# Gathers three jobs ahead with four row buffers, expert weights in natural row order, last job's row loads on Pool's queue, a warm-up for the first gather

## The chip, the cores and the metric

The kernel runs on one core of one Trainium2 chip. The metric is the time of one execution in device microseconds (us); the median of three runs of the kernel before is 736.16 us (733.53 to 736.91). PE is the tensor engine (PEld its weight loads), DVE the vector engine, ACT the scalar engine, POOL the general-purpose engine, SP the engine that only issues transfers. Each engine works off its own instructions in order.

## The reference: one diffusion layer with a mixture of experts

The layer takes 512 tokens of width 1024 and 256 context tokens. First comes a mixer (a combined input projection, a gated short convolution and a gated linear attention, an output projection, a post-norm residual). Then each token goes to two of sixteen experts. What the change touches is the second half:

```python
for e in range(N_EXPERTS):
    act = jax.nn.silu(tok @ w1[e]) * (tok @ w3[e])
    out = out + combine[:, e:e + 1] * (act @ w2[e])
...
x = post_norm_residual(x, hier_moe(modulate(x, sh2, sc2), *moe_w), g2, ln2_g[l], ln2_b[l])
```

`w1` and `w3` are 1024x512 and `w2` is 512x1024 for each expert, all in 32-bit floats; `combine` is zero but for the two experts of a token. `modulate` is x * (1 + scale) + shift, column by column.

## The kernel before, in words

**Jobs.** The kernel sorts the experts by their number of tokens and works through 16 jobs. Two first jobs take up to 96 slots of experts 0 and 1, so that work can start before the sort is known; 14 more have fixed capacities by rank (256, 192, 128 three times, 96 twice, 64 three times, 32 three times, 31), run in the order of `ORDER`, which sets big and small ones in turn: by capacity 96, 96, 31, 256, 32, 192, 64, 128, 64, 128, 64, 128, 96, 96, 32, 31. A job is split into groups of up to 128 slots and each group into blocks. A block of 128 slots (`Block`) splits its weights into a high and a low part (ACT casts `whi`, DVE subtracts `wlo`) and does three products for each; smaller ones (`SmallBlock`) multiply directly in 32 bits. Counting groups there are 18 gathers, counting blocks 21 scatters (the last job has none).

**A job's steps.** `hots` builds the 0/1 matrix of tokens and slots on DVE. `prep` makes the job and calls `slots`: four small matrix products give token numbers and weights per slot, DVE turns them into indices, and an indirect DMA on Pool's queue gathers the token rows from DRAM (`tokd`) into a row buffer `gx` (line 1227). `load` transposes the rows on PE (line 1253) and applies the modulation. `hidden` multiplies with `w1` and `w3`, `gate` does silu and the product, `outputs` multiplies with `w2`, and an indirect DMA on Pool's queue adds the rows to `yd` in DRAM (`scatter`, line 1187). Two scatters both change `yd`, so each waits until the one before has landed.

**The order.** In the loop over the jobs, job n loads the next one's rows within its last hidden step, then does `gate`, then the `prep` of job n+2, then the next job's first hidden step, then its own `outputs`. So on Pool's queue a gather stands between scatters. There are three row buffers. The Tile framework turns the written order into one queue for each engine and moves independent instructions within it.

**Weights.** Each expert comes in six pieces of 1 MB, loaded by SP into a ring of twelve tiles (line 1019), so a piece is issued when the piece of two jobs before has been used, and only in order. The pieces are read with `"o (p k) n -> p (o k) n"`: partition p gets four neighbouring rows of `w1` or two of `w2`, 8 KB in one run. The rows of one product are therefore every fourth (or second) of the matrix, and the kernel compensates: `load` transposes every fourth column of `gx`, `abx` holds the modulation in that order (made by `perm` in `ada_fin` from four extra small loads `pvec`, line 545), and `gate` writes and reads in that order.

**The last job.** `last_hot`, three jobs before the end, builds what adds the last job's rows and ALPHA * `ln1_b` on PE rather than by a scatter. SP loads `ln1_b` into `l1b`, a tile of the ring `ob` of two tiles that also holds the scatters' sources (line 1556); ACT multiplies it by ALPHA (line 1557); SP copies four pieces into `obw` (line 1561), which Pool has set to zero (line 1559). `finish` then reads `yd` back into the three row buffers and one further tile, normalizes and stores.

Of the kernel before, what the change touches and what calls it, by code (L numbers as in the profile page):

```python
# [18 lines left out]
P = 128  # L19
# [35 lines left out]
WARM0, WARM1, WARM2, WARM3 = 28, 8, 16, 16  # L55
# [7 lines left out]
def layer(ctx: ExitStack, tc: tile.TileContext, a, out, dbg=None):  # L63
# [179 lines left out]
    def ada_fin(pa, parts, bank, prio, perm=None):  # L243


        s = sb.tile([P, 512], FT, name="adas", tag="as", bufs=2)
        S.copy(s, pa)
        n = len(parts)

        def columns(src, bias):  # L250
            o = bank()[:, :8 * n].rearrange("p (k q i) -> p q k i", i=2, q=n)
            for j in range(4):
                mm(o[:, :, j, :], src(j), sel[:, 0:2 * n], prio, start=True, stop=True)
            ts_ = []
            for q, (c0, hf) in enumerate(parts):
                t = sb.tile([P, 4, 2], FT, name="adac", tag="adac", bufs=4)
                V.tensor_tensor(t, o[:, q], bias(c0, hf)[:, :, None].to_broadcast([P, 4, 2]), op=OP.add)
                ts_.append(t)
            return ts_

        ts_ = columns(lambda j: s[:, j * P:(j + 1) * P], lambda c0, hf: vc(VBA + 8 * c0, hf))
        if perm:
            return ts_, lambda: columns(lambda j: s.rearrange("r (p c) -> r c p", c=4)[:, j], perm)
        return ts_

    class Ada:
# [10 lines left out]
        def fin(self, perm=None):  # L277
            return ada_fin(self.pa, self.parts, pbg, PR_ADA, perm)
# [7 lines left out]
    def ab_half(dst, sh, sc, hf, g0, b0, col=None):  # L286

        def bc2(c0):
            return (col or vc)(c0, hf)[:, :, None].to_broadcast([P, 4, 2])
# [243 lines left out]
    pvec = sb.tile([P, 4, 2, 4], FT, name="pvec", tag="wsum")  # L533
    V.memset(g4, 0.0)
    with tc.issue_after(wk_lo.ins):
        G.dma_start(wl, dview(a["w_in"], OFF_GF, [[DPROJ, P], [P * DPROJ, KC], [1, 32]]))
        for j in range(4):
            G.dma_start(g4[32 * j:32 * j + 16, :, 0:DK], a["gate_w2_fwd"][0].rearrange("r (h d) -> r h d", h=NH))
            G.dma_start(g4[32 * j + 16:32 * j + 32, :, DK:P], a["gate_w2_bwd"][0].rearrange("r (h d) -> r h d", h=NH))
        G.dma_start(gn, dview(a["gla_norm_g"], 0, [[0, P], [1, DV]]))  # L540
        G.dma_start(wr[:, :, 0:4], a["router_group_w"][0].rearrange("(k p) g -> p k g", p=P))
        G.dma_start(wr[:, :, 4:20], a["router_expert_w"][0].rearrange("(k p) g -> p k g", p=P))

        for n_, v_ in enumerate((a["b_ada"][0, 3 * D:4 * D], a["b_ada"][0, 4 * D:5 * D], a["ln1_g"][0], a["ln1_b"][0])):
            G.dma_start(pvec[:, n_], v_.rearrange("(h p c) -> p h c", h=2, c=4))
        G.dma_start(rb[:, 0:4], dview(a["router_group_b"], 0, [[0, P], [1, 4]]))
        G.dma_start(rb[:, 4:20], dview(a["router_expert_b"], 0, [[0, P], [1, 16]]))
# [33 lines left out]
    ab2 = sb.tile([P, 2, KC, 2], FT, name="ab2", tag="lg")  # L581

    abx = const.tile([P, 2, KC, 2], FT)
# [29 lines left out]
    def px(n, hf):  # L613
        return pvec[:, n, hf]

    (sh0, sc0, sh1, sc1), perm = ada.fin(lambda c0, hf: px(c0 - 3, hf))
# [281 lines left out]
    wsum = sb.tile([P, 2, 20], FT, name="wsum", tag="wsum")  # L898
# [18 lines left out]
    lg = sb.tile([P, NT, 20], FT, name="lg", tag="lg")  # L917
# [265 lines left out]
    gxs = [mo.tile([P, D], FT, name=f"gx{n}") for n in range(3)]  # L1183
# [6 lines left out]

    def every(src, c, j):

        return src.rearrange("s (p c) -> s c p", c=c)[:, j]
# [10 lines left out]
    class Group:  # L1204
# [8 lines left out]
        def slots(self):  # L1213
# [5 lines left out]
            sa = mo.tile([P, 8], FT, name="sa", tag="sa", bufs=8)[:n]  # L1219
            V.tensor_copy(sa[:, :NA], pa[:n, :NA])  # L1220
            V.scalar_tensor_tensor(sa[:, 0:1], sa[:, 2:3], dum[:n, 1:2], sa[:, 0:1], op0=OP.mult, op1=OP.add)
            idx = mo.tile([P, 1], I32, name="idx", tag="idx", bufs=8)[:n]
# [18 lines left out]
        def load(self):  # L1241
# [7 lines left out]
            for hf in range(2):  # L1249
                pt = pt_()  # L1250
                gh = self.g[:, hf * 512:(hf + 1) * 512]
                for c in range(4):
                    PE.transpose(pt[:, c * n:(c + 1) * n], every(gh, 4, c), ident[:n, :n])  # L1253
                v = pt[:, :4 * n].rearrange("p (c n) -> p c n", c=4)
                ks = slice(4 * hf, 4 * hf + 4)
                if big:
                    hi, lo = self.X
                    for c in range(4):
                        A, B = abx[:, 0, 4 * hf + c, 0:1], abx[:, 1, 4 * hf + c, 0:1]
# [6 lines left out]
                else:  # L1266
                    A, B = (abx[:, q, ks, 0:1].to_broadcast([P, 4, n]) for q in range(2))
# [4 lines left out]
    class Block:  # L1272
# [18 lines left out]
        def gate(self):  # L1291
            self.A = hi, lo = hl_tiles(4, "A")
            s_ = mo.tile([P, 512], FT, name="s", tag="s", bufs=3)
            for q in range(2):
                cs = slice(q * 256, (q + 1) * 256)

                h1, h3 = (h[:, cs].rearrange("s (p o) -> s o p", o=2) for h in self.H)
                sq = s_[:, cs].rearrange("s (o p) -> s o p", o=2)
                S.activation(sq, h1, AF.Silu)
                V.scalar_tensor_tensor(sq, h3, self.group.w, sq, op0=OP.mult, op1=OP.mult)  # L1300
                pt = pt_()
                for o in range(2):
                    PE.transpose(pt[:, o * P:(o + 1) * P], sq[:, o], ident)
# [19 lines left out]
    class SmallBlock:  # L1323
# [30 lines left out]
        def gate(self):  # L1354
# [4 lines left out]
            hs = mo.tile([P, 512], FT, name="hs", tag="s", bufs=3)  # L1359
# [109 lines left out]
    for j in seq[:NS]:  # L1469
        ohs[j] = hots(j)  # L1470
        warm(WARM2, pt_)
        prep(j)
    jobs[seq[0]].load()
    with tc.issue_after(jobs[seq[NS - 1]].last.ins):
        for g, n in zip(gxs, [FIRST] * NS + [0]):
            G.memset(g[n:], 0.0)
# [65 lines left out]
    def last_hot():  # L1542
# [7 lines left out]
        V.memset(ohl[:, :, n - 1::n], 1.0)  # L1550
# [15 lines left out]
    for n_, j in enumerate(seq):  # L1566
# [45 lines left out]
    def finish():  # L1612

        ys = gxs + [mo.tile([P, D], FT, name="yf", tag="Xl", bufs=2) for _ in range(1)]
# [121 lines left out]
```

## Time and profile before

| | us |
|---|---|
| median of 3 runs | 736.16 |
| the profiled execution | 739.21 |
| its span, first to last instruction | 737.4 |
| PE busy | 648.9 (88%) |
| DVE busy | 408.0 (55%) |
| ACT busy | 250.5 (34%) |
| POOL busy | 103.9 (14%) |

A busy PE is not a PE at its peak: the ends of pipelined products are modelled, and the clock that PE is granted has two levels, 1.2 and 2.4 GHz (a mean of 0.929 of the full one here). The first 265 us are the mixer, the experts' products run from about 344 to 707 us, `finish` takes the rest. In rows of the timeline the columns are start, duration, engine, line, operation, output and inputs, shape, count, and in brackets how long the engine sat idle before it and what ended that.

### The profile page before, as it was taken

How to read it: one execution, taken by the hardware profiler on the slowest of the kernel's cores; microseconds unless marked ns; L12 is line 12 of the kernel's file. 1: busy time of each engine (PE TensorE's matmuls, PEld its weight loads, DVE VectorE, ACT ScalarE, POOL GpSimd, SP SyncE). 2: the span in 40 equal slices, each digit the busy share in tenths (PEclk: the TensorE clock that was granted, in tenths of full speed). 3: DMA queues.
4: the chain of work that ended last, by engine and by line, in shares of the span. 5: the costliest groups of instructions: out<-in, count | busy, mean ns of one | idle time of the engine just before them, and what ended most of it. 6: DMA issues, size and time to landing. Idle time of an engine off the chain costs nothing.

```text
span 737.4 us, 10628 instructions
## 1 busy us (share of the span) xinstructions
PE 648.9 (88%) x3966; PEld 429.0 (58%) x3966; DVE 408.0 (55%) x1008; ACT 250.5 (34%) x417; POOL 103.9 (14%) x106
## 2 busy tenths in 40 slices
PE   5899999989999999996996898999678978999564
PEld 4465688778887787774443576554444634544321
DVE  7436741685976759558415557456346657312036
ACT  2437712458532325141023444244323453001001
POOL 2330000000000100035103202100210111103102
PEclk8799989999999999997798899899897989999788
DMA  8995955362122098353569798857995989616963
GB/s 302 382 307 179 319 194 172 115 199 88 57 84 89 14 364 335 115 170 132 203 255 405 290 366 275 252 230 244 373 403 176 395 300 335 212 61 227 398 224 116
DMA packets 52984, 172.49 MB, mean 234 GB/s; under 512 B 4477, under 2 KB 17933, under 8 KB 40642
## 3 DMA queue, kind: packets, MB, share of 16 engines
q1 hardware_dynamic: 46130, 157.31, 57.5%
q0 software_dynamic: 5440, 11.27, 7.0%
q10 hardware_dynamic: 1360, 3.21, 1.1%
q8 instruction: 32, 0.52, 0.3%
q14 instruction: 22, 0.18, 0.1%
HBM read 159.88 MB, written 13.50 MB: 235 GB/s over the span
## 4 chain that ended last, share of the span: by engine, by line
PE 57%; DMA 17%; DVE 10%; issue 8%; ACT 5%; POOL 1%; ACTq 0%; SPq 0%; DVEq 0%; POOLq 0%
PE pb L144 22%; PE mm L144 19%; DMA yd<-ob,idx 7%; DMA gx<-tokd,idx 6%; PE gl L144 3%; PE pt L1253 2%; DVE wlo L398 2%; PE bg L146 2%; PE po L144 2%; PE tp L154 1%; DMA x<-in_x_dram 1%; ACT whi L396 1%; DMA raw<-in_w_ada_dram 1%; DVE gg L640 1%; PE bg L160 1%
## 5 line engine op out<-in xcount | busy, mean ns | idle before, releaser
L398 DVE TENSOR_TENSOR wlo<-raw,whi 128x1024 fp32r<-128x1024 f32 x68 | 82.3, 1223 | 62.6 <-ACT whi L396 62.1
L396 ACT CAST whi<-raw 128x1024 fp32r<-128x1024 f32 x68 | 70.7, 1049 | 79.6 <-PE pb L144 50.1
L144 PE MATMUL pb<-ew,xt 128*32 128x256 f32 (+1 forms) x480 | 73.7, 495 | 1.4 <-DVE xt L1270 1.2
L1187 POOL DMA_INDIRECT yd<-ob,idx x21 | 33.9, 1614 | 143.7 <-DVE ob L1388 50.4
L1253 PE MATMUL pt<-ident,gx 128*128 128x128 f32 (+3 forms) x144 | 24.8, 325 | 31.7 <-DMA gx<-tokd,idx 31.7
L144 PE MATMUL pb<-ew,at 128*32 128x256 f32 (+1 forms) x384 | 51.4, 477 | 0.9 <-DVE at L1371 0.5
L144 PE MATMUL pb<-whi,Xh 128*128 128x512 f32 x96 | 42.2, 439 | 6.2 <-ACT Xh L1264 6.2
L1363 ACT COPY hs<-pb 128x256 f32<-128x256 f32 x24 | 8.3, 374 | 114.4 <-PE pb L144 114.4
L144 PE MATMUL mm<-hhi,whi 128*128 128x512 f32 x112 | 44.7, 409 | 2.5 <-ACT hhi L375 2.2
L144 PE MATMUL pb<-raw,xt 128*32 128x256 f32 (+1 forms) x288 | 38.8, 480 | 8.2 <-DMA raw<-in_expert_w_dram 8.2
L1253 PEld LDWEIGHTS pt<-ident,gx 128*128 128x128 f32 (+3 forms) x144 | 21.3, 215 | 39.0 <-issue 28.9
L144 PE MATMUL mm<-hhi,wlo 128*128 128x512 f32 x112 | 43.8, 403 | 0.1
L1227 POOL DMA_INDIRECT gx<-tokd,idx x18 | 20.1, 1114 | 164.1 <-issue 47.0
L144 PE MATMUL mm<-hlo,whi 128*128 128x512 f32 x112 | 42.5, 390 | 0.0
L144 PEld LDWEIGHTS pb<-ew,xt 128*32 128x32 f32 (+1 forms) x480 | 22.4, 127 | 33.7 <-issue 26.2
L144 PE MATMUL pb<-whi,Xl 128*128 128x512 f32 x96 | 41.1, 428 | 0.0
L144 PE MATMUL pb<-wlo,Xh 128*128 128x512 f32 x96 | 41.0, 427 | 0.0
L144 PE MATMUL mm<-wlo,hhi 128*128 128x256 f32 x128 | 37.9, 296 | 0.0
L144 PE MATMUL mm<-whi,hhi 128*128 128x256 f32 x128 | 37.9, 296 | 0.0
L144 PE MATMUL mm<-whi,hlo 128*128 128x256 f32 x128 | 37.6, 294 | 0.0
L144 PEld LDWEIGHTS pb<-ew,at 128*32 128x32 f32 (+1 forms) x384 | 18.5, 125 | 28.8 <-issue 23.6
L301 POOL TENSOR_TENSOR ss<-ss,nhalf 128x4 f32<-128x4 f32 x4 | 5.4, 1358 | 192.3 <-DVE ss L300 192.3
(431 smaller groups left out, 1374.9 us busy)
## 6 DMA issues: line engine op xcount, KB each, us to landing
ew<-in_expert_w_dram SPq DMA_DIRECT2D x64, 1024.0 KB, 7.1
raw<-in_expert_w_dram SPq DMA_DIRECT2D x32, 1024.0 KB, 10.7
raw<-in_w_ada_dram SPq DMA_DIRECT2D x22, 1024.0 KB, 10.7
raw<-in_w_in_dram SPq DMA_DIRECT2D x10, 1024.0 KB, 6.3
raw<-in_w_out_dram SPq DMA_DIRECT2D x4, 1024.0 KB, 4.9
xz<-in_x_dram SPq DMA_DIRECT2D x4, 512.0 KB
ada<-in_w_ada_dram SPq DMA_DIRECT2D x2, 1024.0 KB
x<-in_x_dram SPq DMA_DIRECT2D x4, 512.0 KB, 11.3
```

What stands on the lines that cost most here:

```text
L144: return PE.matmul(o, lhsT, rhs, **kw)
L146: return PE.matmul(o, lhsT, rhs, **kw)
L154: PE.transpose(pool_tile[:, j * P:(j + 1) * P], s, ident)
L160: PE.transpose(o[:, :P], ident, ident)
L301: pows.append(G.tensor_tensor(dst, dst, nhalf[:, :dst.shape[1]], op=OP.pow))
L396: S.copy(hi, r[:, k0:k0 + step, :])
L398: lows.append(lo_eng[k0 // step].tensor_tensor(lo, r[:, k0:k0 + step, :], hi.bitcast(FT), op=OP.subtract))
L640: V.tensor_tensor_scan(g[DK:P, ::-1], mask[DK:P, :n], m[DK:P, ::-1], 0.0, op0=OP.mult, op1=OP.add)
L1187: G.indirect_dma_start(out=yd.rearrange("t (r w) -> (t r) w", r=R), out_offset=bass.IndirectOffsetOnAxis(ap=idx[:, :1], axis=0), in_=o, in ...
L1227: self.last = G.indirect_dma_start(out=self.g, out_offset=None, in_=tokd, in_offset=bass.IndirectOffsetOnAxis(ap=idx[:, :1], axis=0), **kw)
L1253: PE.transpose(pt[:, c * n:(c + 1) * n], every(gh, 4, c), ident[:n, :n])
L1363: S.copy(hs[:, cs].rearrange("s (o p) -> s o p", o=2), self.ph[:, cs].rearrange("s (p o) -> s o p", o=2))
```

## The change

Gathers: `prep` of job n+3 (was n+2) and `hots` of job n+4 (was n+3) after the `gate` of job n, also for the first jobs; four row buffers (was three). Tile counts go down: `sa` and `idx` 8 to 6, `s` 3 to 2, `sg` 2 to 1. Weight pieces: partition p gets rows p, p+128, ..., so runs of 2 KB for `w1` and `w3` and of 4 KB for `w2`; the compensation goes (`abx`, `pvec`, `perm`, `every`, the strided views in `gate`). Last job: ALPHA goes into the 0/1 matrix, and the four row pieces come straight from `ln1_b` by DMAs on Pool's queue; `finish` uses the four row buffers. Warm-up: 34 transposes on PE between the first two gathers' issue and the first `load`.

```diff
-WARM0, WARM1, WARM2, WARM3 = 28, 8, 16, 16
+WARM0, WARM1, WARM2, WARM4 = 28, 8, 16, 34
...
-        for n_, v_ in enumerate((a["b_ada"][0, 3 * D:4 * D], a["b_ada"][0, 4 * D:5 * D], a["ln1_g"][0], a["ln1_b"][0])):
-            G.dma_start(pvec[:, n_], v_.rearrange("(h p c) -> p h c", h=2, c=4))
...
-    xp = perm()
-    ab_half(abx, xp[0], xp[1], 0, 2, 3, px)
-    ab_half(abx, xp[2], xp[3], 1, 2, 3, px)
...
-        return src.rearrange("o (p k) n -> p (o k) n", p=P)
+        return src.rearrange("o (k p) n -> p (o k) n", p=P)
...
-    gxs = [mo.tile([P, D], FT, name=f"gx{n}") for n in range(3)]
+    gxs = [mo.tile([P, D], FT, name=f"gx{n}") for n in range(4)]
...
-                    PE.transpose(pt[:, c * n:(c + 1) * n], every(gh, 4, c), ident[:n, :n])
+                    PE.transpose(pt[:, c * n:(c + 1) * n], gh[:, c * P:(c + 1) * P], ident[:n, :n])
...
-            for q in range(m // 2):
-                cs = slice(q * 256, (q + 1) * 256)
-                S.copy(hs[:, cs].rearrange("s (o p) -> s o p", o=2), self.ph[:, cs].rearrange("s (p o) -> s o p", o=2))
-            sg = mo.tile([P, 4, n], FT, name="sg", tag="sg", bufs=2)
+            S.copy(hs[:, :m * P], self.ph[:, :m * P])
+            sg = mo.tile([P, 4, n], FT, name="sg", tag="sg", bufs=1)
...
+    warm(WARM4, pt_)
     jobs[seq[0]].load()
...
-        V.memset(ohl[:, :, n - 1::n], 1.0)
+        V.memset(ohl[:, :, n - 1::n], ALPHA)
...
-        l1b = mo.tile([1, D], FT, name="l1b", tag="ob", bufs=2)
-        nc.sync.dma_start(l1b, dview(a["ln1_b"], 0, [[0, 1], [1, D]]))
-        S.activation(l1b, l1b, AF.Copy, scale=ALPHA)
...
-            nc.sync.dma_start(obw[(q + 1) * n - 1:(q + 1) * n, q * w:(q + 1) * w], l1b[:, q * w:(q + 1) * w])
+            G.dma_start(obw[(q + 1) * n - 1:(q + 1) * n, q * w:(q + 1) * w], dview(a["ln1_b"], q * w, [[0, 1], [1, w]]))
...
-        if n_ + 3 < len(seq) and n_ + 3 >= NS + 2:
-            ohs[seq[n_ + 3]] = hots(seq[n_ + 3])
-        if n_ + 2 < len(seq) and n_ + 2 > NS:
-            prep(seq[n_ + 2])
+        if n_ + 4 < len(seq):
+            ohs[seq[n_ + 4]] = hots(seq[n_ + 4])
+        if n_ + 3 < len(seq):
+            prep(seq[n_ + 3])
...
-        ys = gxs + [mo.tile([P, D], FT, name="yf", tag="Xl", bufs=2) for _ in range(1)]
+        ys = gxs
```

## Rows read from the trace of the kernel before

**Rows 1.** The page's chain that ended last: shares of the span by engine.

```profile
PE 57%; DMA 17%; DVE 10%; issue 8%; ACT 5%; POOL 1%; ACTq 0%; SPq 0%; DVEq 0%; POOLq 0%
```

**Rows 2.** Stretches: length, busy us by engine, PE's granted clock, DMA share, GB/s.

```profile
500.00:635.00 135.00, 112.68 (x495) 63.30 (x492) 78.42 (x175) 48.49 (x72) 18.42 (x14) 0.91 0.89 328
635.00:684.00 49.00, 46.76 (x379) 22.09 (x377) 12.40 (x47) 5.56 (x15) 8.17 (x6) 1.00 0.44 138
684.00:707.50 23.50, 12.15 (x136) 7.41 (x134) 3.44 (x13) 1.27 (x5) 3.10 (x2) 0.78 0.96 364
```

**Rows 3.** Waits (total us, times, longest), then PE's timeline around gathers.

```profile
PE pt L1253 <- DMA gx<-tokd,idx: 31.7, 7, 7.4
...
529.02 1.22 PE L1253 MATMUL pt<-ident,gx 64*128 64x64 f32 x8 [7.36 <-DMA gx<-tokd,idx]
...
534.54 3.65 PE L144 MATMUL pb<-ew,xt 128*64 128x512 f32 x14
...
595.42 1.95 PE L1253 MATMUL pt<-ident,gx 128*128 128x128 f32 x8 [4.52 <-DMA gx<-tokd,idx]
597.30 5.71 PE L144 MATMUL pb<-ew,xt 128*64 128x512 f32 x14
```

**Rows 4.** Timeline of POOL: a scatter and the gather behind it.

```profile
516.76 1.57 POOL L1187 DMA_INDIRECT yd<-ob,idx  x1 [12.27 <-DMA yd<-ob,idx]
518.63 1.00 POOL L1227 DMA_INDIRECT gx<-tokd,idx  x1 [0.30 <-issue]
```

**Rows 5.** SP's own waits (total us, times, longest), and its timeline.

```profile
SPq L1561 <- ACT l1b L1557: 20.6, 1, 20.6
SPq L1556 <- DMA yd<-ob,idx: 19.5, 1, 19.5
...
670.58 2.81 SPq L1019 DMA_DIRECT2D ew<-in_expert_w_dram  x5
```

**Rows 6.** PE's timeline near the end of the jobs.

```profile
691.49 0.64 PE L144 MATMUL pb<-raw,xt 128*32 128x256 f32 x2 [6.95 <-DMA raw<-in_expert_w_dram]
```

**Rows 7.** The chain in order of time (start, us, what): its last scatters.

```profile
664.20 4.92 DMA yd<-ob,idx
...
699.80 7.75 DMA yd<-ob,idx
```

**Rows 8.** Transfers: landing (us), stretches as in rows 2, a queue of the page.

```profile
raw<-in_w_out_dram SPq DMA_DIRECT2D x4, 1024.0 KB, 4.9
...
DMA to landing us min/median/max: 5.0/5.0/5.0
...
30.00:34.00 4.00, 1.84 (x13) 1.20 (x11) 2.99 (x5) 1.72 (x3) 4.00 (x4) 1.00 1.05 388
435.00:439.00 4.00, 4.00 (x19) 3.19 (x18) 1.68 (x6) 0.74 (x1) 0.00 (x0) 1.00 1.02 416
...
q0 software_dynamic: 5440, 11.27, 7.0%
```

**Rows 9.** Groups by form: busy us and mean ns; then PE's timeline.

```profile
L1253 PEld LDWEIGHTS pt<-ident,gx 128*128 128x128 f32 x48 | 8.5, 218 | 18.9 <-issue 18.4 <-DVE Xl L1196 0.4
L154 PEld LDWEIGHTS pt<-ident,hs 128*128 128x128 f32 x48 | 5.4, 143 | 5.1 <-ACT hs L1363 2.8 <-issue 1.0 <-DVE Xl L1196 0.7
L545 POOL DMA_DIRECT2D pvec<-in_b_ada_dram x2 | 1.4, 739 | 0.0
...
93.97 1.85 PE L146 MATMUL bg<-sel,adas 128*128 128x8 f32 x8
```

**Rows 10.** PE's timeline at the first two loads, from the warm-up before.

```profile
337.14 1.97 PE L160 MATMUL pt<-ident 128*128 128x128 f32 x16
...
344.07 1.53 PE L1253 MATMUL pt<-ident,gx 96*128 96x96 f32 x8 [4.83 <-DMA gx<-tokd,idx]
354.72 5.91 PE L144 MATMUL pb<-ew,xt 128*64 128x512 f32 x38
361.70 5.52 PE L144 MATMUL pb<-ew,xt 128*64 128x512 f32 x48
```

More of the change, by code (lines that the diff above doesn't have):

```diff
@@ L241, in ada_mm, with ada_fin @@
                start=q == 0 and half == 0, stop=last and half == 1)
-    def ada_fin(pa, parts, bank, prio, perm=None):
+    def ada_fin(pa, parts, bank, prio):
         s = sb.tile([P, 512], FT, name="adas", tag="as", bufs=2)
@@ L248, in ada_fin @@
         n = len(parts)
[L250 to L263, printed above, removed]
+        o = bank()[:, :8 * n].rearrange("p (k q i) -> p q k i", i=2, q=n)
+        for j in range(4):
+            mm(o[:, :, j, :], s[:, j * P:(j + 1) * P], sel[:, 0:2 * n], prio, start=True, stop=True)
+        ts_ = []
+        for q, (c0, hf) in enumerate(parts):
+            t = sb.tile([P, 4, 2], FT, name="adac", tag="adac", bufs=4)
+            V.tensor_tensor(t, o[:, q], vc(VBA + 8 * c0, hf)[:, :, None].to_broadcast([P, 4, 2]), op=OP.add)
+            ts_.append(t)
         return ts_
@@ L275, in add, with fin @@
                 ada_mm(self.pa, r, half, PR_ADA, len(self.parts) - 1, len(self.parts) == self.n)
-        def fin(self, perm=None):
-            return ada_fin(self.pa, self.parts, pbg, PR_ADA, perm)
+        def fin(self):
+            return ada_fin(self.pa, self.parts, pbg, PR_ADA)
     ab = sb.tile([P, 2, KC, 2], FT, name="ab")
@@ L532, in layer @@
     rb = sb.tile([P, 20], FT, name="rb")
-    pvec = sb.tile([P, 4, 2, 4], FT, name="pvec", tag="wsum")
     V.memset(g4, 0.0)
@@ L577, in layer @@
     lowC = gate_low(zcT, CT)
-    ab2 = sb.tile([P, 2, KC, 2], FT, name="ab2", tag="lg")
-    abx = const.tile([P, 2, KC, 2], FT)
+    ab2 = const.tile([P, 2, KC, 2], FT)
     gT = const.tile([P, 2, KC], FT)
@@ L897, in layer @@
     V.memset(onesf, 1.0)
-    wsum = sb.tile([P, 2, 20], FT, name="wsum", tag="wsum")
+    wsum = sb.tile([P, 2, 20], FT, name="wsum")
     for q, w_ in enumerate((wa, wr)):
@@ L916, in layer @@
         S.dma_start(yd[T:T + P, h * 512:(h + 1) * 512], zero)
-    lg = sb.tile([P, NT, 20], FT, name="lg", tag="lg")
+    lg = sb.tile([P, NT, 20], FT, name="lg")
     st1 = sb.tile([P, NT, 3, 6], FT, name="st1")
@@ L1218, in slots @@
                 mm(pa[:n, :NA], self.oh[:, i, :n], self.auxj(i), start=i == 0, stop=i == NT - 1)
-            sa = mo.tile([P, 8], FT, name="sa", tag="sa", bufs=8)[:n]
+            sa = mo.tile([P, 8], FT, name="sa", tag="sa", bufs=6)[:n]
             V.tensor_copy(sa[:, :NA], pa[:n, :NA])
             V.scalar_tensor_tensor(sa[:, 0:1], sa[:, 2:3], dum[:n, 1:2], sa[:, 0:1], op0=OP.mult, op1=OP.add)
-            idx = mo.tile([P, 1], I32, name="idx", tag="idx", bufs=8)[:n]
+            idx = mo.tile([P, 1], I32, name="idx", tag="idx", bufs=6)[:n]
             V.tensor_scalar(idx, sa[:, 0:1], sa[:, 1:2], dum[:n, 0:1], op0=OP.add, op1=OP.add)
@@ L1266, in load @@
                 else:
-                    A, B = (abx[:, q, ks, 0:1].to_broadcast([P, 4, n]) for q in range(2))
+                    A, B = (ab2[:, q, ks, 0:1].to_broadcast([P, 4, n]) for q in range(2))
                     x = self.xt[:, ks, :n]
@@ L1292, in gate @@
             self.A = hi, lo = hl_tiles(4, "A")
-            s_ = mo.tile([P, 512], FT, name="s", tag="s", bufs=3)
+            s_ = mo.tile([P, 512], FT, name="s", tag="s", bufs=2)
             for q in range(2):
                 cs = slice(q * 256, (q + 1) * 256)
[L1297 to L1300, printed above, removed]
+                S.activation(s_[:, cs], self.H[0][:, cs], AF.Silu)
+                V.scalar_tensor_tensor(s_[:, cs], self.H[1][:, cs], self.group.w, s_[:, cs], op0=OP.mult, op1=OP.mult)
                 pt = pt_()
-                for o in range(2):
-                    PE.transpose(pt[:, o * P:(o + 1) * P], sq[:, o], ident)
+                transpose4(pt, [s_[:, q * 256 + o * P:q * 256 + (o + 1) * P] for o in range(2)])
                 v = pt[:, :2 * P].rearrange("p (k t) -> p k t", k=2)
@@ L1472, in layer @@
         prep(j)
+    warm(WARM4, pt_)
     jobs[seq[0]].load()
     with tc.issue_after(jobs[seq[NS - 1]].last.ins):
-        for g, n in zip(gxs, [FIRST] * NS + [0]):
+        for g, n in zip(gxs, [FIRST] * NS + [0, 0]):
             G.memset(g[n:], 0.0)
```

14 lines of the change are left out of this document (5 added, 9 removed).

## The prediction, made before the changed kernel was run

> **What bounds the kernel now.** I began with the page's chain that ended last. PE holds 57% of it, but DMA holds 17% [rows 1], and that share is the one this change can reach: the chain written out in order of time shows DMA almost only as gathers between 339 and 630 us and as five scatters in a row at the end. So two places are in question.
>
> The first is PE's wait for gathered rows. In the list of waits, PE's transposes stood idle for gathers 31.7 us in seven waits; the timeline shows them at big and small jobs alike [rows 3]. Why the rows are late stands on Pool's queue: a scatter waited 12.27 us until the scatter before it had landed, and the gather written behind it left at 518.63 [rows 4]; PE could use its rows at 529.02 [rows 3], 10.4 us later. The gather itself asks for nothing that a job earlier wasn't known.
>
> The second is the end. SP's own waits name two of about 20 us, one for a scatter to land (line 1556 needs a tile of the ring that holds the scatters' sources) and one for ACT (line 1557, queued behind work of ACT's own), and only at 670.58 does SP go on with weights [rows 5]. These 40 us fall into the stretch 635 to 684, where PE is full at full clock and the transfers are busy 0.44 of the time; in the next stretch it is the reverse, 0.96 for the transfers and 12.15 us of PE in 23.5 [rows 2]. PE pays at 691.49: 6.95 us for weights [rows 6]. And the five scatters that close the jobs, 664.20 to 707.55, take 4.92 us at first and 8.71, 9.69, 8.82 and 7.75 us once the late weights run beside them [rows 7].
>
> **The change, part by part.** Durations are those of the profiled execution, 739.2 us (span 737.4 and 1.8 around it), which lies 3.0 us above the median of 736.16.
>
> *Gathers a job earlier.* The first wait (4.83 us, [rows 10]) stays; the others are 31.7 - 4.83 = 26.9 us. A job in this phase is some 22 us (the 135 us of the first stretch hold about six, [rows 2]). The longest remaining wait is 7.36 us, so a gather that leaves one job earlier is in time with over 10 us to spare, even behind the same scatter. I take -26.9 (between -20 and -26.9). The new wait is the one for a row buffer: with two groups in the biggest jobs, three jobs ahead hold at most three groups at once plus the one being transposed, and the buffer that is taken was transposed in the hidden step just before, so I cost it at nothing; without that cover a gather would wait for a transpose, and behind it on Pool's queue the scatter of the job in hand. The moved DVE work (one-hot matrices, indices) is the same in number. The smaller counts of `sa`, `idx`, `s` and `sg` cost at most some tenths of a microsecond in the jobs with two small blocks; I take 0.
>
> *The clock after the waits.* After the gather of 595.42 the run of 14 small products took 5.71 us against 3.65 at full clock [rows 3]: 2.1 us lost, for the eight transposes perhaps 0.8 more. Four waits are of 4.5 us or more, so about 2.5 x 4 = 10 us. Some of it will come back, since after the transposes of a big job ACT and DVE need time for the modulation and the split before PE can use them: -8 (0 to -11).
>
> *Weights in natural order.* Runs of 2 KB (64 pieces, 67.1 MB) and 4 KB (32 pieces, 33.6 MB) for runs of 8 KB. The trace has loads with 2 KB runs, of `w_out` and `w_ada`. Alone, the 1 MB of `w_out` lands in 4.9 us, and the expert load that was timed between 436 and 480 us, with 8 KB runs, in 5.0: no price. In a full stream they differ: 388 GB/s at a share of 1.05 against 416 at 1.02 [rows 8], so 370 and 408 GB/s for a full share. That makes 67.1 x (1/0.370 - 1/0.408) = 16.9 us of transfer time, and 4.2 for `w2` at half the difference: 0 to 21 us over 16 jobs. What of it lies on the path depends on the stretch: 500 to 635 us has a share of 0.89, so 120 us of transfers, plus up to 8 for its six jobs; PE without its four waits there (two of them stand in rows 3, together they are 19.4 us) and the slow clock (three of them, 7.5) would be done in 108. Transfers and PE then come out nearly equal. The ring's lead (up to two jobs) gives the transfers some slack, and in the stretch behind it they are half idle. I take +8, between 0 and +20.
>
> The Trainium skill, page "DMA: Bandwidth & Descriptors", section "Why small descriptors are slow (HBM only)", speaks against this part: each packet costs about 3 fixed cycles beside its 32-byte beats. By it 2 KB runs need 67/64 and 8 KB runs 259/256, 3.5% more time per byte; an estimate from that page is 6 us for `w1` and `w3`, less than the row's 16.9. With it the sum would be some 4 us better.
>
> *The compensation goes.* Weight loads from every fourth column take 218 ns, from neighbouring ones 143 [rows 9]: 75 ns x 144 = 10.8 us of PEld, nearly all beside PE. Eight transposes at full clock differ by some 0.1 us, 18 times: -2 (0 to -5). The second set of column products in `ada_fin` is a PE item of 1.85 us in a full stretch [rows 9]: -1.7. Four `pvec` loads of 0.74 us leave Pool, where nobody waits: 0.
>
> *The first gather.* The warm-up of 34 transposes, at the 16 in 1.97 us of the warm-up before it, takes 4.2 us and fits into the 4.83 us of idling. What it can save is the half clock after: from 345.6 to 360.6 us PE needed 15 us for 48 products that take 5.52 the second time [rows 10]; I put 2 to 3 of it down to table products and a wait for DVE between them. So 0 to -7; DVE is slow there too, so I take -4. Were the clock to fall anyway the warm-up would last twice as long: +3.
>
> *The last job's rows.* SP's 40 us of standing go, the four DMAs go to Pool's queue at 0.74 us each as `pvec` did [rows 9], at a time when Pool is idle. Weights of the last two jobs come while PE is full. PE saves 6.95 [rows 6] and, as after a gather, some 2.5 at half clock. The scatters go back to about 4.9 us plus 0.7 between them: the last three, from 677.3, when their products are ready, end at 677.3 + 3 x 5.6 = 694, or 696 by PE, against 707.55 [rows 7]. I take -12; if scatters stay at 9 us it is -3, and -14 is the most.
>
> The same page's section "Issuing engines are not separate DMA queues" says that moving a DMA to another issuing engine saves only the time to issue it. By that rule this part would be worth 2.5 us or less on SP and the sum 12 us worse. Rows 5 show what the rule leaves out: the issuing engine was held by waits of its own.
>
> **The sum.** -26.9 - 8 + 8 - 2 - 1.7 - 4 - 12 = -46.6. 739.2 - 46.6 = 692.6, and with the 3.0 us between this execution and the median 689.6: **690 us**. With every bound at its best it is about 671, at its worst (waits -20, clock 0, transfers +20, strides 0, warm-up +3, tail -3) about 734; either end needs all of them together.
>
> **The rivals.** *Transfers become the bound* (0.20). The waits go, and PE then waits for weights: +20 in place of +8, and nothing from the first gather. 690 + 12 + 4 = 706. For it: the share of 0.89 [rows 2]. Against it: PE's one long wait for weights is that of rows 6, after SP's standing.
>
> *The tail stays* (0.14). The scatters must still follow one another, and the weights still run beside them: 690 + 9 = 699.
>
> *The gathers don't come earlier* (0.05). Pool's order puts them behind scatters that wait [rows 4], or the row buffer is late. Then only the tail, the warm-up and the compensation count: 736 - 12 - 4 - 4 + 2 = 718. Against it: the gather goes with its job's place in the loop.
>
> *Slower: packets, not bytes, set the pace* (0.06). The software queue moved 5440 packets, 11.27 MB, in 7.0% of 16 engines' span [rows 8]: 826 us of engine time, 152 ns for 2.07 KB, which is 218 GB/s. If 2 KB runs went at that pace, `w1` and `w3` of the 14 later jobs (58.7 MB) would take 269 us, `w2` (29.4 MB, halfway between the rates) 94, the software queue its 52: 415 us in the 363 from the first load of rows (344.07, [rows 10]) to 707.55. That ends 52 us late: 736 + 52 = 788. It decides from a rate below about 260 GB/s on; against it stand 388 GB/s for such runs [rows 8].
>
> **How the numbers follow.** The forecast's case has 0.52; 0.03 is left for no change at all. The forecast, full transfers, the staying tail and the late gathers are all faster, 0.91. About 0.5% (3.7 us) is what a measurement here can tell from no change: within it 0.03, slower 0.06. The range runs from 675, near the best bounds, to 716, which takes in the cases of 699 and 706 with 10 us to spare and leaves out the late gathers, no change and the slow packets: 0.14, and some 0.05 below.
>
> **What would show it.** Right: PE's waits for gathers shrink to the first one, of about 0.5 to 1 us beside the warm-up; gathers stand on Pool's queue a job earlier; SP has no wait at `last_hot`, and the share in the stretch with the two jobs of 96 rises over 0.44; scatters at the end take 5 to 6 us; PEld at line 1253 about 143 ns. Wrong: waits of PE or ACT for expert weights by tens of microseconds, or a DMA share at 1.0 all through with fewer GB/s than 370 (transfers); a last chain of scatters at 9 us each (tail); gathers that still end waits (order); a clock of 0.5 after the first load in spite of the warm-up.

## The result, and the profile after

The changed kernel took **685.31 us** (median of 4 runs, 680.76 to 688.91) and the kernel before, beside it, 736.53 us (733.53 to 738.34): ratio 0.9305, interval 0.9241 to 0.9369. In a second set it was 684.72 against 734.09 us, ratio 0.9345 (0.9292 to 0.9397). The forecast was 690, with a range of 675 to 716. The sum was nearly met, but two of its terms were far off, in opposite directions, and a third has no trace behind it; the experiments below show which.

The profiled execution of the changed kernel took 688.91 us (span 687.1), and the mean granted clock rose from 0.929 to 0.955. In the page's chain by engine, DMA has half of its share of before and PE more [rows 1]:

```profile
PE 67%; DVE 13%; DMA 9%; ACT 6%; issue 2%; POOL 1%; ACTq 0%; SPq 0%; DVEq 0%
```

The gathers are gone from the list of PE's waits; it was led by 31.7 us for them [rows 3]. What leads it now (total us, times, longest):

```profile
PE pb L144 <- ACT Xh L1241: 10.3, 3, 4.6
PE py L144 <- DMA gx<-yd: 8.9, 1, 8.9
PE bg L160 <- DVE dum L1036: 4.1, 1, 4.1
```

Stretches of the changed kernel (columns as in rows 2: length, busy us of PE, PEld, DVE, ACT, POOL, PE's clock, DMA share, GB/s). The jobs end some 50 us sooner, so 600 to 640 is where 635 to 684 stood before:

```profile
380.00:500.00 120.00, 114.33 (x681) 69.90 (x682) 75.03 (x166) 49.71 (x79) 19.19 (x15) 0.93 0.91 308
500.00:600.00 100.00, 93.70 (x446) 56.37 (x444) 68.37 (x152) 41.52 (x58) 19.14 (x17) 0.97 1.05 371
600.00:640.00 40.00, 39.99 (x348) 16.39 (x344) 10.10 (x39) 4.17 (x11) 7.20 (x5) 1.00 1.04 368
640.00:660.00 20.00, 9.63 (x144) 5.21 (x136) 3.69 (x13) 1.64 (x6) 3.10 (x2) 0.90 0.73 243
```

The hole in the transfers (0.44 in 635:684, [rows 2]) is filled: share 1.04 while PE is full at full clock. For 140 us the transfers have a share of 1.04 to 1.05, the highest that these rows and rows 8 show, and PE is still busy for 0.94 and 1.00 of the two stretches. SP's timeline and Pool's show what filled it (start, duration, what, count):

```profile
600.05 21.97 SPq L1000 DMA_DIRECT2D ew<-in_expert_w_dram  x5
622.22 8.30 SPq L1000 DMA_DIRECT2D raw<-in_expert_w_dram  x4
637.04 1.24 SPq L1000 DMA_DIRECT2D ew<-in_expert_w_dram  x2
```

```profile
557.57 1.02 POOL L1204 DMA_INDIRECT gx<-tokd,idx  x1 [14.06 <-DVE cmp L1637]
562.45 1.56 POOL L1168 DMA_INDIRECT yd<-ob,idx  x1 [3.86 <-DVE ob L1293]
565.27 2.09 POOL L1529 DMA_DIRECT2D obw<-in_ln_b_dram  x4 [0.30 <-POOL obw L1527]
```

The last weights leave at 637.04; before, SP still had five loads and more to send at 670.58 [rows 5]; the four row loads cost Pool 2.09 us at a place where it is idle. PE's timeline answers to rows 3 and 10:

```profile
336.88 0.85 PE L1230 MATMUL pt<-ident,gx 96*128 96x96 f32 x8 [1.06 <-DVE oh L1160]
522.09 3.65 PE L144 MATMUL pb<-ew,xt 128*64 128x512 f32 x14
530.34 0.79 PE L144 MATMUL pb<-whi,Xh 128*128 128x512 f32 x1 [4.60 <-ACT Xh L1241]
```

Ahead of the first load PE stands for 1.06 us, put down to DVE (4.83 us before, put down to the gather). The 14 small products behind a gather take 3.65 us, the time at full clock. But at 530.34 PE waits 4.60 us for ACT's split of the rows: part of the gathers' wait has moved one step on in the big jobs (10.3 us in all, 6.2 before).

The whole stretch of the experts, from the first load of rows to the landing of the last scatter (columns as in rows 2), in the kernel before, in the changed kernel, and in a second profile of the changed kernel (r1_after):

```profile
344.07:707.55 363.48, 315.29 (x1916) 175.78 (x1916) 176.79 (x440) 105.26 (x178) 60.54 (x48) 0.91 0.77 280
336.88:656.23 319.35, 299.25 (x1916) 166.16 (x1916) 174.60 (x435) 103.60 (x169) 62.12 (x53) 0.95 0.92 319
335.96:647.69 311.73, 291.60 (x1916) 162.30 (x1916) 175.78 (x437) 103.64 (x169) 62.53 (x53) 0.98 0.94 327
```

The first number behind the length is PE's busy time; the rest of the length is PE's idling. It falls from 48.2 us to 20.1 in both profiles of the changed kernel. These two differ by 7.7 us in the busy time of the same 1916 products, at a clock of 0.95 and of 0.98: between these two executions it is the clock that differs and not PE's idling, so idling is the steadier figure to compare here.

### The profile page after: what moved, and what is told of

Read it like the earlier page. It is cut to its first block, busy times and chain, and to the rows that moved or that the text cites. A ratio compares the mean times of both kernels' runs of the same rounds, so it can differ in the third digit from the quotient of the medians.

```text
span 687.1 us, 10650 instructions
## 1 busy us (share of the span) xinstructions
PE 631.7 (92%) x3992; PEld 419.3 (61%) x3992; DVE 405.7 (59%) x998; ACT 248.6 (36%) x408; POOL 102.5 (15%) x107
## 4 chain that ended last, share of the span: by engine, by line
PE 67%; DVE 13%; DMA 9%; ACT 6%; issue 2%; POOL 1%; ACTq 0%; SPq 0%; DVEq 0%
PE pb L144 31%; PE mm L144 22%; DMA raw<-in_expert_w_dram 4%; DVE wlo L391 3%; PE gl L144 2%; DMA raw<-in_w_ada_dram 2%; PE po L144 2%; ACT whi L389 2%; PE bg L146 2%; PE pt L154 1%; PE pt L1230 1%; PE tp L154 1%; PE py L144 1%; DVE gg L621 1%; PE ptb L144 1%
## 5 line engine op out<-in xcount | busy, mean ns | idle before, releaser
L144 PE MATMUL pb<-ew,xt 128*32 128x256 f32 (+1 forms) x480 | 66.9, 470 | 0.2 <-DVE xt L1247 0.2
L144 PE MATMUL pb<-whi,Xh 128*128 128x512 f32 x96 | 42.4, 442 | 10.3 <-ACT Xh L1241 10.3
L144 PE MATMUL pb<-ew,at 128*32 128x256 f32 (+1 forms) x384 | 48.7, 464 | 0.7 <-DVE at L1341 0.7
L1333 ACT COPY hs<-pb 128x512 f32<-128x512 f32 (+1 forms) x16 | 7.7, 479 | 93.1 <-PE pb L144 93.1
L1204 POOL DMA_INDIRECT gx<-tokd,idx x18 | 18.7, 1036 | 146.4 <-DVE idx L1200 39.6
L144 PEld LDWEIGHTS pb<-ew,xt 128*32 128x32 f32 (+1 forms) x480 | 21.6, 121 | 29.7 <-issue 23.7
L144 PE MATMUL mm<-wlo,hhi 128*128 128x256 f32 x128 | 37.5, 293 | 0.0
L144 PEld LDWEIGHTS pb<-ew,at 128*32 128x32 f32 (+1 forms) x384 | 16.8, 120 | 26.7 <-issue 20.9
L144 PEld LDWEIGHTS pb<-whi,Xh 128*128 128x128 f32 x96 | 19.5, 203 | 21.6 <-ACT Xh L1241 12.1
L391 DVE TENSOR_TENSOR wlo<-ew,whi 128x1024 fp32r<-128x1024 f32 x20 | 24.4, 1221 | 10.0 <-ACT whi L389 10.0
```

The source lines that it names most:

```text
L144: return PE.matmul(o, lhsT, rhs, **kw)
L391: lows.append(lo_eng[k0 // step].tensor_tensor(lo, r[:, k0:k0 + step, :], hi.bitcast(FT), op=OP.subtract))
L1204: self.last = G.indirect_dma_start(out=self.g, out_offset=None, in_=tokd, in_offset=bass.IndirectOffsetOnAxis(ap=idx[:, :1], axis=0), **kw)
L1333: S.copy(hs[:, :m * P], self.ph[:, :m * P])
```

## The experiments

What a part is worth was asked in two ways: put back into the changed kernel (against 684.72 us in the first set, and ratios 0.9305 and 0.9345), and made alone in the kernel before. Three runs (r5, r7, r9) change one side of the row order and leave out the other, so their products are of mismatched rows, though the same in number. Differences in us are those of medians within a set, unless a ratio is named; by the ratios of the table, r2, r3 and r4 are 9, 17 and 8 us slower than the changed kernel, where the medians give 11.6, 17.8 and 11.8. A difference between sets stands to about 4 us.

| run | what it is | us | ratio to before, interval |
|---|---|---|---|
| r1_after | the changed kernel | 684.72 | 0.9345, 0.9292 to 0.9397 |
| r2_w8k | weights and compensation put back | 696.31 | 0.9471, 0.9420 to 0.9523 |
| r3_prep_late | gathers put back | 702.52 | 0.9570, 0.9512 to 0.9627 |
| r4_tail_sp | last job's rows put back | 696.49 | 0.9456, 0.9384 to 0.9527 |
| r5_runs8k | only the 8 KB runs put back | 690.79 | 0.9425, 0.9386 to 0.9464 |
| r6_early | only the early compensation put back | 691.98 | 0.9401, 0.9350 to 0.9452 |
| r7_strided | only the strides put back | 687.36 | 0.9394, 0.9355 to 0.9434 |
| r8_nowarm | warm-up taken out | 688.59 | 0.9397, 0.9361 to 0.9433 |
| r9_only_runs2k | before, only shorter runs | 718.56 | 0.9787, 0.9742 to 0.9832 |
| r10_only_order | before, only the weights' part | 712.69 | 0.9686, 0.9625 to 0.9748 |
| r11_only_gather | before, only the gathers | 704.97 | 0.9604, 0.9556 to 0.9652 |
| r12_only_tail | before, only the last job's rows | 725.52 | 0.9888, 0.9838 to 0.9938 |

### The reference of the first set

r1_after, no edit.

> The changed kernel as it is, beside which the other three of this set are read. It took 685.31 us against 736.53 us; here again 683 to 689 us, 0.93 of the kernel before.

684.72 us. Its profiled execution was a quick one (span 676.8, clock 0.974), 10 us below the other profile of the same kernel (687.1, clock 0.955): a single profile's span proves nothing below that.

### The weights' part put back

```diff
-        return src.rearrange("o (k p) n -> p (o k) n", p=P)
+        return src.rearrange("o (p k) n -> p (o k) n", p=P)
...
+    (sh0, sc0, sh1, sc1), perm = ada.fin(lambda c0, hf: px(c0 - 3, hf))
...
-  PE.transpose(pt[:, c * n:(c + 1) * n], gh[:, c * P:(c + 1) * P], ident[:n, :n])
+  PE.transpose(pt[:, c * n:(c + 1) * n], every(gh, 4, c), ident[:n, :n])
```

> The changed kernel with only the weight loads put back: 8 KB runs and the compensating strided token views, so every weight TensorE load of the up-projection is strided again (218 ns each against 140 ns now). Theory: the 2 KB runs cost transfer time only where the queues are full. In 500:640 us of the changed kernel the transfers have a busy share of 1.04 to 1.05 at 368 to 371 GB/s, where the kernel before moved 416 GB/s at 1.02. With 8 KB runs the same bytes would go a tenth faster there, some 14 us of transfer time in 140 us, of which TensorE, busy for 0.94 of 500:600, can use 5 to 15: 670 to 680 us. Rival A: the runs cost nothing, as the landings of single pieces had it (4.9 us against 5.0), and the strided loads cost the 2 to 5 us that the compensation took: 687 to 691 us. Rival B: the slow weight loads of 218 ns are the larger effect once TensorE is the bound for 0.92 of the span: over 695 us.

11.6 us slower than the changed kernel, where the first theory had it faster; only rival B's number, over 695, is met. So the natural order, for which the forecast had charged 8 us less 3.7, is a gain. The theory's premise held: 380 GB/s at a share of 1.02 in 500:600. What didn't follow was that PE would profit.

### Gathers put back

```diff
-        if n_ + 3 < len(seq):
-            prep(seq[n_ + 3])
+        if n_ + 2 < len(seq) and n_ + 2 > NS:
+            prep(seq[n_ + 2])
```

> The changed kernel with its gathers issued as late as before (two jobs ahead, three row buffers), all else as changed. Theory: the gathers' waits on TensorE come back, 31.7 us in the kernel before, of which 20 to 27 us showed in the span, and the half clock after them: 705 to 712 us. Rival: the transfers set the pace of 500:640 us anyway (share 1.04 to 1.05), so the wait would only have been moved from the weights to the gathers: 685 to 695 us.

17.8 us slower, between the rival's range and the theory's 705 to 712: the waits are back, and transfers at a share of 1.05 in 500:600 did not hide them. But they are back at little more than half their size:

```profile
PE pt L1230 <- DMA gx<-tokd,idx: 15.6, 6, 3.8
```

That is 11.3 us less than the 26.9 that this part had to give in the kernel before [rows 3], at the same place in the loop. Something else in the change had already shortened them.

### The last job's rows put back

```diff
-            G.dma_start(obw[...], dview(a["ln1_b"], q * w, [[0, 1], [1, w]]))
+            nc.sync.dma_start(obw[...], l1b[:, q * w:(q + 1) * w])
```

> The changed kernel with the last job's row loads put back on SyncE's queue behind the wait for the rows, all else as changed. Theory: SyncE stands still for some 20 us again and the loads of the last jobs' weights queue behind it, as in 635:684 us of the kernel before, where the transfers' share fell to 0.44; TensorE then waits for weights at the end: 697 to 705 us. Rival: SyncE's stand was hidden behind the gathers' waits and is short without them; only the issue itself returns: 686 to 690 us.

11.8 us slower by the medians, 8 by the ratios, half a microsecond below the first theory's range and well above the rival's. SP stands between the two loads again, ahead of the last jobs' weights:

```profile
607.23 0.33 SPq L1527 DMA_DIRECT2D l1b<-in_ln_b_dram  x1
607.81 0.40 SPq L1000 DMA_DIRECT2D ew<-in_expert_w_dram  x1
624.24 2.53 SPq L1532 DMA_DIRECT2D obw<-l1b  x4
...
645.44 4.20 SPq L1000 DMA_DIRECT2D ew<-in_expert_w_dram  x2
```

```profile
600.00:640.00 40.00, 36.16 (x313) 15.70 (x313) 7.48 (x31) 5.12 (x12) 5.65 (x4) 0.99 0.65 207
640.00:660.00 20.00, 12.84 (x131) 7.05 (x123) 1.12 (x5) 1.19 (x4) 3.10 (x2) 0.76 1.05 384
```

The share falls to 0.65 and the catching up comes in 640:660, at a PE clock of 0.76. The last job's weights leave at 645.44 in place of 637.04, and PE waits 10.5 us for expert weights in four waits, where its list in the changed kernel names none.

### Run length alone, in the changed kernel

```diff
-        return src.rearrange("o (k p) n -> p (o k) n", p=P)
+        return src.rearrange("o (p k) n -> p (o k) n", p=P)
```

> The changed kernel with the expert weights loaded in runs of 8 KB again and nothing else: the rows of a piece then stand in another order than the tokens' columns, so the products are of mismatched rows; the work is the same. It measures the run length by itself. The kernel with 8 KB runs and its compensation was 11.6 us slower than the changed kernel. Theory: the length of a run is worth little or a little for 8 KB (TensorE had idle weights nowhere in 500:600 either way; 380 GB/s at share 1.02 against 369 at 1.05), and the 11.6 us are the compensation: 678 to 685 us, 0 to 6 faster than the changed kernel. Rival: 2 KB runs are themselves what made the weights faster: 690 to 697 us.

690.79 us, a ratio 0.008 to 0.012 above the changed kernel's: 6 to 9 us slower, as the rival had it, not faster. The longer runs did move bytes faster, and nothing came of it:

```profile
500.00:600.00 100.00, 96.08 (x461) 56.20 (x463) 70.04 (x158) 41.89 (x59) 21.00 (x18) 0.97 1.02 390
```

390 GB/s at 1.02 is 382 for a full share, against 371 at 1.05, 353: 8% a byte (6% by r2_w8k and r1_after: 380 at 1.02 against 369 at 1.05), close to the 10% that the forecast took from rows 8. The Trainium skill, page "DMA: Bandwidth & Descriptors", section "Why small descriptors are slow (HBM only)", has 3.5% by its fixed cycles for each packet, and 4.6% with the 32 bytes of descriptor data for each run that it also names (both estimates); here the loss is larger, and it is off the path all the same. Where these 6 to 9 us are lost its profile does not show (span 685.3, inside the changed kernel's own spread; PE idles 21 us in the stretch of the experts, the changed kernel 20); that stays open.

### The early compensation alone

```diff
+        for n_, v_ in enumerate((a["b_ada"][0, 3 * D:4 * D], ...)):
+            G.dma_start(pvec[:, n_], v_.rearrange("(h p c) -> p h c", h=2, c=4))
...
+    xp = perm()
+    ab_half(abx, xp[0], xp[1], 0, 2, 3, px)
```

> The changed kernel with the compensation's early part added back and nothing else: the four loads of single biases in pieces of 16 bytes on Pool's queue at the start, the second set of columns from the condition's products, and the second pair of scales (its result is read by nobody here). Theory: this is half of the 11.6 us. The first load of a routed or shared expert's weights stood at 255.6 and 256.0 us in the two kernels that have it and at 247.2 to 250.2 us in the four that don't: 5 to 8 us slower than the changed kernel, 690 to 693 us, and that load at 255 us. Rival: the difference at the start is chance between two executions, and only the four matmuls and their columns stay, as forecast 1.7 us: 686 to 687 us.

691.98 us, a ratio 0.006 to 0.010 above: 4 to 7 us, hardly clear of the 4 us between sets, but over the forecast's 1.7. The first load of an expert's weights is a good mark for this part. In the six kernels that have it, it stands at 253.3 to 256.1 us, in the eight without it at 247.2 to 250.2, and not one overlaps: 6.1 us between the means. Some 2.5 us of it are here, in PE's timeline:

```profile
91.78 1.06 PE L146 MATMUL bg<-sel,adas 128*128 128x8 f32 x8 [1.31 <-ACT adas L247]
...
93.81 0.41 PE L144 MATMUL mm<-wlo,hhi 128*128 128x256 f32 x1
94.03 0.41 PE L144 MATMUL mm<-whi,hlo 128*128 128x256 f32 x1
94.24 1.85 PE L146 MATMUL bg<-sel,adas 128*128 128x8 f32 x8
...
98.86 0.41 PE L144 MATMUL mm<-wlo,hhi 128*128 128x256 f32 x1
...
99.80 0.28 PE L144 MATMUL mm<-whi,hhi 128*128 128x256 f32 x1
```

The second set of eight products takes 1.85 us (the first 1.06) because it falls into a time of half clock, and the full clock (0.28 in place of 0.41 a product) is back only at 99.7: 7.9 us after the first set began, with 24 of these products done. In the changed kernel the clock falls behind the first set too (88.40), and the same 24 are done 5.4 us after it. In 85:100 the granted clock was 0.77 in the kernel before and 0.89 in the changed one. The forecast counted the eight products and not that the half clock lasts longer. Of the rest, 2.2 us stand there by 20 us: the first products of `sel` and `adas` start at 22.1 to 23.5 us in the six and at 19.4 to 21.6 in the eight, and PE's granted clock in 15:20 is 0.50 to 0.66 in the six and 0.73 to 1.00 in the eight. That is long before this part's first instruction, the `pvec` loads (41.7), so this part's work can't have caused it; whether it is chance between executions is not shown.

### The strides alone

```diff
-  PE.transpose(pt[:, c * n:(c + 1) * n], gh[:, c * P:(c + 1) * P], ident[:n, :n])
+  PE.transpose(pt[:, c * n:(c + 1) * n], every(gh, 4, c), ident[:n, :n])
...
-            S.copy(hs[:, :m * P], self.ph[:, :m * P])
+            for q in range(m // 2):
+                S.copy(hs[:, cs].rearrange(...), self.ph[:, cs].rearrange(...))
```

> The changed kernel with the strided views added back and nothing else (transposes that read every fourth column of the gathered rows, the hidden layer's columns by pairs, two half copies of it): the tokens' columns are then in another order than the weights' rows, the work is the same. Theory: the 144 transposes of the gathered rows were 22.0 us of TensorE with the strides and 16.6 without, TensorE is the bound for nine tenths of the span, and the half copies lengthen the way from one job to the next: 4 to 7 us slower than the changed kernel, 689 to 692 us. Rival: the strides hide behind the other work: within 2 us, 683 to 687 us.

687.36 us, between the two theories; the ratio is 0.005 to 0.009 above, 4 to 7 us, hardly clear of the 4 us between sets. PE's transposes of gathered rows, mean of one:

```profile
L1234 PE MATMUL pt<-ident,gx 128*128 128x128 f32 (+3 forms) x144 | 21.7, 291 | 0.9 <-DVE oh L1160 0.9
```

They took 17.0 us (261 ns) in the profile of the changed kernel, so 4.7 us of PE; the forecast's bounds, 0 to 5, hold by the trace.

### No warm-up

```diff
-    warm(WARM4, pt_)
```

> The changed kernel without the 34 transposes ahead of the first gathered rows. Theory: TensorE then stands for some 5 us at that place and comes back at half clock, as in the kernel before; in the profile of the changed kernel the stretch from the shared expert's first load to the next job's was 14.8 us against 16.5: 2 to 4 us slower, 687 to 689 us. Rival: the clock fell there all the same (0.50 in 339:347 us) and the transposes only fill a wait: within 1.5 us, 683 to 686 us.

688.59 us, as the first theory had it: 3.9 us above 684.72, and by the ratios 4 to 7, hardly clear of the 4 us between sets. The wait is back whole, here from the second gather's table products to the second load of rows, and then the changed kernel at the same place:

```profile
331.06 0.30 PE L144 MATMUL psl<-aux,oh 128*96 128x6 bf16 x4
336.13 1.51 PE L1230 MATMUL pt<-ident,gx 96*128 96x96 f32 x8 [4.76 <-DMA gx<-tokd,idx]
...
350.68 0.88 PE L1230 MATMUL pt<-ident,gx 96*128 96x96 f32 x8
```

```profile
331.67 0.30 PE L144 MATMUL psl<-aux,oh 128*96 128x6 bf16 x4
...
351.63 0.88 PE L1230 MATMUL pt<-ident,gx 96*128 96x96 f32 x8
```

That is 19.6 us without the warm-up and 20.0 with it. In all eight profiles with the warm-up it is 17.5 to 20.5 us, in the mean 19.6 as well, and in r11_only_gather, without it, 19.4. So the 4 us are not to be found at the place where the warm-up should give them, and that they come from it is not shown.

### Run length alone, in the kernel before

```diff
-        return src.rearrange("o (p k) n -> p (o k) n", p=P)
+        return src.rearrange("o (k p) n -> p (o k) n", p=P)
```

> The kernel before with the expert weights loaded in natural row order, runs of 2 KB (4 KB for w2) and nothing else: rows and columns are mismatched, the work is the same. The opposite of the run with 8 KB runs in the changed kernel, which was some 6 us slower than the changed kernel, against the forecast's term of +8 for the 2 KB runs. Theory: shorter runs are harmless or a help, as that run had it: 726 to 733 us. Rival: they cost where the queues are full (the forecast's term, 0 to +20): 738 to 745 us.

718.56 us, 14.3 us **faster** than the kernel before: the forecast's sign was wrong, and even the theory here asked for less. PE's waits say where it comes from:

```profile
PE pt L1253 <- DMA gx<-tokd,idx: 18.0, 6, 4.7
PE pb L144 <- DMA raw<-in_expert_w_dram: 8.6, 2, 6.9
```

31.7 - 18.0 = 13.7 us of the gathers' waits are gone, though no gather was moved in the program, and in the stretch of the experts PE idles 35.0 us in place of 48.2. One of them, on Pool and on PE:

```profile
505.83 2.55 POOL L1187 DMA_INDIRECT yd<-ob,idx  x1 [9.09 <-DVE oh L1179]
508.68 1.00 POOL L1227 DMA_INDIRECT gx<-tokd,idx  x1 [0.30 <-issue]
```

```profile
515.96 1.17 PE L1253 MATMUL pt<-ident,gx 64*128 64x64 f32 x8 [2.04 <-DMA gx<-tokd,idx]
```

In the kernel before, the scatter in front of this gather waited 12.27 us for an earlier scatter to land [rows 4], and PE 7.36 us for the rows [rows 3]. Here the scatter waits for DVE, PE for 2.04 us, and from the gather's start to PE's it takes 7.3 us in place of 10.4. The slowest of the indirect transfers land sooner. For the gathers' landing (us), first the kernel before, then this one, then the changed kernel, then the changed kernel with 8 KB runs:

```profile
DMA to landing us min/median/max: 2.5/6.7/12.3
```

```profile
DMA to landing us min/median/max: 2.4/7.1/8.0
```

```profile
DMA to landing us min/median/max: 2.4/5.8/7.8
```

```profile
DMA to landing us min/median/max: 2.5/6.5/12.0
```

The median hardly differs; the longest does. Over all 14 profiles, the longest landing of a gather is 11.2 to 12.6 us in the five kernels with 8 KB runs and 7.7 to 9.6 in the nine with shorter ones, and a scatter's median 9.0 to 10.0 against 7.9 to 8.8. That gathers wait their turn behind long packets of the weights fits this, but is argued: no run here varies anything of the packets but the length of the run. That fewer bytes of weights are under way at a time, since SP is held longer at each issue (last section), would fit as well; no run separates the two.

### The weights' part alone, in the kernel before

The edit is that of r2_w8k, the other way round, with the two work tiles at two and one buffers.

> The kernel before with the weights' natural order and all of the compensation gone (early loads and columns, strided views), nothing else. Theory: the early part is worth about 4 us, the strides about 4, the runs nothing or some us, as in the changed kernel, where putting all three back cost 11.6 us: 720 to 728 us. Rival: the forecast's sum of +8 for the runs, -2 and -1.7 for the compensation: 736 to 741 us.

712.69 us: 20.2 us faster than before, more than the theory had (720 to 728), and 5.9 faster than the shorter runs alone. Its waits for gathers are 18.9 us, much as in the run before it; the 5.9 us are the compensation, where r6 and r7 together had some 8 to 14 with the uncertainty of two sets.

### The gathers alone, in the kernel before

The edit is that of r3_prep_late, the other way round, with the fourth buffer and the two work tiles at two and one buffers.

> The kernel before with the gathers three jobs ahead and a fourth buffer (and, to have the room, two and one buffers in place of three and two for two work tiles, as the changed kernel has), nothing else. Theory: the waits of 31.7 us go, and of them 18 us show, as they did when the later gathers were put back into the changed kernel: 712 to 718 us. Rival A, the forecast's terms, -26.9 and -8 by the clock: 699 to 706 us. Rival B: without the row loads moved, SyncE's wait stands at the end in place of the gathers: 725 to 734 us.

704.97 us, 27.9 us faster: more than put back (17.8), as rival A had it. Of the waits only the first is left, and some of it comes back at ACT:

```profile
PE pb L144 <- ACT Xh L1264: 9.6, 3, 4.9
...
PE pt L1253 <- DMA gx<-tokd,idx: 4.7, 1, 4.7
```

SP's standing did not take the gathers' place (rival B). The stretch of the experts, to be read beside the first of the three rows in the section on the result:

```profile
339.88:668.95 329.07, 302.70 (x1916) 171.82 (x1916) 176.35 (x440) 105.27 (x178) 62.05 (x49) 0.95 0.84 309
```

PE idles 26.4 us in place of 48.2, and the same products keep it busy 12.6 us less, at a clock of 0.95 in place of 0.91. These two executions lie 37.5 us apart, though, 9.6 more than the medians of their sets, so how the 27.9 us divide between idling and clock can't be read from them.

### The last job's rows alone, in the kernel before

The edit is that of r4_tail_sp, the other way round.

> The kernel before with only the last job's row loads on Pool's queue. Theory: SyncE no longer stands for 20.6 us ahead of the last jobs' weights, and the transfers of 635:684 us (share 0.44) are pulled ahead: 722 to 727 us, as putting the wait back into the changed kernel cost 11.8 us. Rival: with the gathers still late, TensorE has not consumed the buffers that these weights need, so the stand is hidden: 732 to 736 us.

725.52 us, 7.3 us faster, as the theory had it. The stretch that had a share of 0.44 [rows 2] now reads:

```profile
635.00:684.00 49.00, 46.75 (x444) 20.98 (x442) 10.68 (x46) 5.07 (x16) 7.27 (x7) 1.00 0.76 262
```

No version that leaves out a part beats the changed kernel.

## Why the prediction was right, and where it was wrong

**The order of the stages was read rightly**: the two places, gathers and end, were the places. Two terms came out near their price. *The last job's rows*: -12 forecast, 8 to 12 put back, 7 to 8 alone (that the late gathers leave PE less to gain from early weights there is argued). By the rule of the Trainium skill's page "DMA: Bandwidth & Descriptors", section "Issuing engines are not separate DMA queues", another issuing engine would have been worth the issue time, 2.5 us; r4 shows that the standing in line on SP is what was paid for. *The strides*: -2 forecast (0 to -5), some 4 to 7 measured, and 4.7 us of PE in the trace.

*The warm-up* met its number, -4 forecast and about 4 measured, but not its mechanism. The half clock that it was to save, the forecast's own sign of being wrong, came all the same: in 339:347 the clock was 0.50 in one profile of the changed kernel and 0.79 in the other, and 0.67 without the warm-up. The stretch up to the second load of rows is as long without the warm-up as with it. What the 4 us are, if they are more than noise, is open.

**The step that failed is "weights in natural order", "+8, between 0 and +20".** Alone it was worth -14.3 us. The forecast's rate per byte was right (10% forecast, 8% seen); that a slower stream lies on the path was not. And its bounds excluded a gain with no reason given: it looked at what the slower stream costs the weights, and took the landing of the gathers beside it as given. Most of the gain is there: 13.7 us of PE's waits for gathers are gone.

**The gathers' term was then too large**: -26.9 and -8 for the clock. Alone it was 27.9 us of these 34.9. Of the rest, 3.4 us went to longer waits for ACT's split (9.6 against 6.2), which the forecast had put into the clock's term; whether the waits or the clock fell short beyond that isn't shown, since the trace has the higher clock (r11_only_gather). Beside the shorter runs it was 17.8, since the two parts take the same waits: 31.7 us, of which the runs take 13.7 and the earlier gathers the rest. Summed in the order runs, rest of the weights' part, gathers, last rows, warm-up, the measured steps are -14.3 - 5.9 - 17.8 - 11.8 - 3.9 = -53.7, against -49 to -51 measured whole and -46.6 forecast; each of these steps stands to some 4 us. So that the forecast came within 5 us is luck: two errors of 22 and 17 us almost cancelled, -26.9 - 8 + 8 = -26.9 forecast for runs and gathers, -14.3 - 17.8 = -32.1 measured.

**The ada columns** were worth 4 to 7 us, not 1.7. The trace shows 2.5 us: the term counted eight products and not that the half clock lasts longer by them. The rest lies in part ahead of this part's first instruction and is not shown to be its work.

**The rivals.** *Transfers become the bound* came true in part of the trace and not in the time: 500 to 640 us has a share of 1.04 to 1.05 and the chain has two stretches on expert weights (30.3 us, from 374.50 and 505.86), but no wait for them stands in PE's list, and a faster stream (r5_runs8k) made nothing faster. *The tail stays*: no; the last scatter landed at 656.2, 3.68 us after it left (7.75 before, [rows 7]). *Gathers not earlier*: no. *Packets set the pace*: no; 371 GB/s is far over the 260 at which it would have decided.

## What to carry to other kernels

Two parts that attack the same wait must not be added: ask what is left of a wait after each. When the shape of a big transfer changes, look for the small transfers that run beside it, and at their longest landing: here it moved from 12.3 us to 8.0 while the median hardly did, and on Pool's queue all that stands behind a late scatter waits with it. And a wait of a queue's issuing engine for something else is a cost to all that is queued behind it, whatever the transfer itself costs. Last, a term whose number is met is not yet a mechanism that is met: ask the trace for the place.

## What the runs showed that was not expected

Shorter runs slowed the stream (353 against 382 GB/s for a full share) and sped up the kernel, while gathers landed at most 8.0 us after their start instead of 12.3 and scatters at most 10.4 instead of 13.1 (r9_only_runs2k against the kernel before). They also lengthened the issue itself on SP. Expert loads into `raw`, ns (minimum, median, longest), in the changed kernel and with 8 KB runs put back:

```profile
L1000 SPq DMA_DIRECT2D raw<-in_expert_w_dram x32: 368/1087/8716, 250.2 to 628.3; - x32
```

```profile
L1000 SPq DMA_DIRECT2D raw<-in_expert_w_dram x32: 328/333/783, 248.0 to 624.3; - x32
```

A median of 1.1 us against 0.33, and up to 8.7 us, with nothing named that it waited for; what is queued behind on SP has to bear that. The clock at the first load fell in spite of the warm-up: it was 1.00 in 332:337 of the changed kernel, and after two waits of 1.06 and 1.36 us it was 0.50 in 339:347, where PE was busy for 7.73 of the 8 us (0.79 there in r1_after).
